# Where in SBUF the halves of the weights lie, modulo 256 bytes, in a hybrid attention and S5 block

## The chip, the cores and the metric

The kernel runs on one core of one Trainium2 chip. The metric is the time of one execution in device microseconds (us), as the median of several runs.

## The reference

One decoder block over 256 tokens of width 1024, all in float32:

```
h = rms_norm(x, norm_mix_g)
q, k, v, u, g = split(h @ w_in)          # 8 heads of 128; u: 512 wide; g: two gates of 1024
o_a = causal softmax attention(rotary(q), rotary(k), v)   # 256 tokens are one MoBA block
o_b = s5_branch(u)                       # complex diagonal scan, gelu, then GLU with w_glu
mixed = sigmoid(g_a) * o_a + sigmoid(g_b) * o_b
x = x + mixed @ w_out
h = rms_norm(x, norm_mlp_g)
x = x + square(relu(h @ w_up)) @ w_down  # 1024 -> 4096 -> 1024
return rms_norm(x, norm_final_g)
```

## The kernel before

Every large product keeps float32 precision by splitting both factors into two halves in the matmul type float32r: hi is a copy in that type, made by ScalarE (line 88), and lo is the rest, made by VectorE (line 89). A product is then three matmuls, hi by hi, hi by lo and lo by hi.

The weights come in units of 128 x 1024 float32 (512 KB). A unit is loaded by the SP queue into one of five `raw` buffers and split into one of four `hi` and one of four `lo` buffers. TensorE uses the units in two ways:

- Stationary weights, 256 columns moving (`mm3`, lines 93 to 95, and line 184 for u): q, k and the gates g of the in-projection and the up stage. The 128x128 pieces of the unit are loaded into the array and x's parts, 256 tokens, move. One unit is 24 matmuls.
- Moving weights, 512 columns (`tok_mm`, lines 270 to 272, and `down`, lines 737 to 739): v, the second gate gb, GLU, merge (w_out, tile names wo) and down. Here the activations' parts are the stationary data. One unit is 12 matmuls. In the second half of down the tokens of the second half (tile names dnq) are done in two pieces of 256 columns, 12 more matmuls for 6 of the 512 wide ones.

The activations' halves are: `xgh`, `xgl` (x times its norm's weights) for the in-projection; the same place under the names `x2h`, `x2l` for up; `yhl` for GLU; `mxh`, `mxl` for merge; `hh`, `hl` for down.

The order of units is V, the S5 preparation, q, k and g of four pairs of heads with attention in between, gb, GLU (four units of columns), merge, up (16 pairs of units), down (two halves of 16 units). TensorE takes its instructions in that order, mixed with the matmuls of attention and S5 as a planner has laid them. In up pairs 0 and 1 are interleaved by the planner, from pair 2 on the units follow one another. In the second half of down the last four units are held back (`LAST = 4`) and their pieces ordered by output.

The addresses. Tiles of a pool lie one behind the other in the order of their first use, each rounded up to 32 bytes a partition. `keep` holds, among others, at these bytes of a partition in the compiled program: half_pi 41920, quarter 41952, xgh and x2h 41984, xgl and x2l 50176, the four hi buffers 58368, 62528, 66688 and 70848, the four lo buffers 75008, 79168, 83328 and 87488, mxh 91648, mxl 99840. The pools ph1 and ph2 follow at 108032: yhl 118272, hh 120320, hl 153088. Modulo 256, x's parts, yhl, mxh, mxl, hh and hl are at 0. A hi or lo buffer has 64 bytes more than the data (`SHIFT = 16` float32), so the four hi buffers are at 0, 64, 128 and 192, and the four lo buffers too. The two halves of a unit always have the same place. Each offset inside a tile that a matmul uses is a multiple of 256 bytes (or of 512), so the place of a tile modulo 256 is that of every piece.

Which buffer a unit gets is fixed by the order in which buffers come free. In up from pair 2 on, and in down, the units have the places 64, 192, 0, 128 in turn. The second unit of the second k pair (tile k, from about 86.9 us) has 64.

Of the kernel before, what the change touches and what calls it, by code (L numbers as in the profile page):

```python
# [8 lines left out]
F32 = mybir.dt.float32  # L9
F32R = mybir.dt.float32r  # L10
# [6 lines left out]
P = 128  # L17
# [16 lines left out]
TURN = 2.0 * math.pi  # L34

RAW, HI, LO = 5, 4, 4
SHIFT = 16
SPLIT_PRIO = 800
HEAT = 7
RSP = 600  # L40
# [9 lines left out]
def build(ctx, tc, dr, out):  # L50
    nc = tc.nc
    V, S, G, PE = nc.vector, nc.scalar, nc.gpsimd, nc.tensor

    keep = ctx.enter_context(tc.tile_pool(name="keep", bufs=1))
# [14 lines left out]
    def w_load(src, name):  # L69
        raw = keep.tile([P, 1024], F32, tag="raw", bufs=RAW, name=f"raw_{name}")  # L70
        nc.sync.dma_start(raw, src)
        return raw

    def parts(name):

        return [keep.tile([P, 1024 + SHIFT], F32R, tag=tag, bufs=bufs, name=f"{tag}_{name}")[:, 0:1024]
                for tag, bufs in (("hi", HI), ("lo", LO))]

    def w_unit(src, name, raw=None):
        if raw is None:  # L80
            raw = w_load(src, name)
        hi, lo = parts(name)
        with tc.high_priority(SPLIT_PRIO):
            split(hi, lo, raw)
        return hi, lo

    def split(hi, lo, x):
        ins = S.copy(hi, x).ins  # L88
        V.tensor_sub(lo, x, hi.bitcast(F32))  # L89
        return ins  # L90
# [56 lines left out]
    ident, tri = cst[:, 640:768], cst[:, 768:896]  # L147
    ones = keep.tile([P, 1], F32, name="ones")
    V.memset(ones, 1.0)
    half_pi = keep.tile([P, 1], F32, name="half_pi")  # L150
    V.memset(half_pi, math.pi / 2)
    quarter = keep.tile([P, 1], F32, name="quarter")
    V.memset(quarter, 0.25)
    heat = p1.tile([P, 512], BF16, tag="sw", name="heat")
    V.memset(heat, 0.0)
    hot = att_bank("hot").rearrange("p a b -> p (a b)")
# [3 lines left out]

    xgh = keep.tile([P, KD, T], F32R, tag="xh", name="xgh")
    xgl = keep.tile([P, KD, T], F32R, tag="xl", name="xgl")
    sq = p1.tile([P, KD, T], F32, tag="yhl", name="sq")
    u_acc = ps.tile([P, 2, 2, T], F32, tag="x", name="u_acc")
    for c in range(4):
        wh, wl = parts(f"u{c}")
        for k2 in range(2):
            k, cols = 2 * c + k2, slice(k2 * 512, (k2 + 1) * 512)
            xk = xT[:, k, :] if k else x0
            S.activation(xgh[:, k, :], xk, AF.Copy, scale=g_mix[:, k : k + 1])  # L170
            V.scalar_tensor_tensor(xgl[:, k, :], xk, g_mix[:, k : k + 1],
                                   xgh[:, k, :].bitcast(F32), op0=ALU.mult, op1=ALU.subtract)
            if k:
                last = split(wh[:, cols], wl[:, cols], u_raw[c][:, cols])
                if k == 1:
                    second = last
            else:
                for i in range(2):
                    part = slice(i * 256, (i + 1) * 256)
                    split(wh[:, part], wl[:, part], u_raw[c][:, part])  # L180
            ws = [slice(k2 * 512 + m * P, k2 * 512 + (m + 1) * P) for m in range(4)]
            for i, (w, x) in enumerate(((wh, xgh), (wh, xgl), (wl, xgh))):
                for m in range(4):
                    PE.matmul(u_acc[:, m // 2, m % 2, :], w[:, ws[m]], x[:, k, :],
                              start=(k == 0 and i == 0 and m % 2 == 0),
                              stop=(k == KD - 1 and i == 2), skip_group_check=True)
# [41 lines left out]
    u = p1.tile([P, 4, 2, P], F32, name="u")  # L228
# [18 lines left out]
    def in_unit(i, name):  # L247
        return w_unit(dr["w_in"][i], f"{name}_{i}", early.get(i))
# [356 lines left out]
    for step in ORDER.split():  # L605
# [28 lines left out]
        elif part == "B":  # L634
            for i in range(2):
                thb[2 * n + i] = p1.tile([P, 2, T], F32, tag=("cs", "sn")[n], bufs=4,
                                         name=f"thb{2 * n + i}")
# [10 lines left out]
    for q in range(4):  # L648
        acc = wide_banks(f"glu{q}") if q % 2 else [flat(mm_bank(f"glu{q}{h}")) for h in range(2)]
        for kk_ in range(2):  # L650
            wh, wl = w_unit(dr["w_glu"][2 * q + kk_], f"glu{q}{kk_}")
            for k2 in range(2):
                k, w = 2 * kk_ + k2, slice(k2 * 512, (k2 + 1) * 512)
                for hf in range(2):
                    tok_mm(acc[hf], wh[:, w], wl[:, w], yhl[0][:, 0:4], yhl[0][:, 4:8], k, hf,
                           k == 0, k == 3)
        tp = att_bank(f"mt{q}")
        for hf in range(2):
            sg = p1.tile([P, T], F32, tag=f"ab{hf}", name="sg")
            act(sg, acc[hf][:, 256:512], AF.Tanh, scale=0.5)  # L660
            V.scalar_tensor_tensor(sg, sg, 1.0, acc[hf][:, 0:256], op0=ALU.add, op1=ALU.mult)
            tb = thb[q][:, hf, :]
            V.scalar_tensor_tensor(tb, tb, 1.0, sg, op0=ALU.add, op1=ALU.mult)
            for i in range(2):
                PE.transpose(tp[:, i, hf * P : (hf + 1) * P], tb[:, i * P : (i + 1) * P], ident)
        two = slice(2 * q, 2 * q + 2)
        V.scalar_tensor_tensor(mixA[:, two, :], tp, 0.5, mixA[:, two, :],
                               op0=ALU.mult, op1=ALU.add)
        split(mxh[:, two, :], mxl[:, two, :], mixA[:, two, :])
# [12 lines left out]
    for c in range(2):  # L682
        acc = wide_banks(f"wo{c}") if c else [flat(mm_bank(f"wo{c}{h}")) for h in range(2)]
        for kk_ in range(4):
            wh, wl = w_unit(dr["w_out"][c, kk_], f"wo{c}{kk_}")
            for k2 in range(2):
                k, w = 2 * kk_ + k2, slice(k2 * 512, (k2 + 1) * 512)
                for hf in range(2):
                    tok_mm(acc[hf], wh[:, w], wl[:, w], mxh, mxl, k, hf, k == 0, k == KD - 1)
        tps = [att_bank(f"xt{c}{i}") for i in range(2)]  # L690
        for hf in range(2):
            xc = x2t[:, hf, c * 512 : (c + 1) * 512]
            V.scalar_tensor_tensor(xc, acc[hf], 0.5, xc, op0=ALU.mult, op1=ALU.add)
            for i in range(4):
                PE.transpose(tps[i // 2][:, i % 2, hf * P : (hf + 1) * P],
                             xc[:, i * P : (i + 1) * P], ident)
        for i in range(4):
            m, tp = 4 * c + i, tps[i // 2][:, i % 2, :]
            S.activation(x2h[:, m, :], tp, AF.Copy, scale=g_mlp[:, m : m + 1])
            V.scalar_tensor_tensor(x2l[:, m, :], tp, g_mlp[:, m : m + 1],  # L700
                                   x2h[:, m, :].bitcast(F32), op0=ALU.mult, op1=ALU.subtract)
# [70 lines left out]
    for c in range(2):  # L772
# [4 lines left out]
        for kk_ in range(16):  # L777
            wh, wl = w_unit(dr["w_down"][c, kk_], f"dn{c}{kk_}")
# [105 lines left out]
```

## Time and profile before

| | |
|---|---|
| median of 3 runs | 403.47 us (402.77 to 404.03) |
| the profiled execution | 403.71 us |
| its span, first to last instruction | 401.9 us |
| mean granted TensorE clock (share of full speed) | 0.999 |
| busy: TensorE matmul / weight loads | 391.6 us / 351.2 us |
| busy: VectorE / ScalarE / GpSimd | 292.6 / 226.0 / 29.2 us |

A profile is of one execution, and its times count from the first instruction. Matmuls are pipelined: a matmul's record lasts two to three times as long as the time until the next one starts, so the busy time of TensorE says little on its pace. The pace is read from the starts.

### The profile page before, as it was taken

How to read it: one execution, taken by the hardware profiler on the slowest of the kernel's cores; microseconds unless marked ns; L12 is line 12 of the kernel's file. 1: busy time of each engine (PE TensorE's matmuls, PEld its weight loads, DVE VectorE, ACT ScalarE, POOL GpSimd, SP SyncE). 2: the span in 40 equal slices, each digit the busy share in tenths (PEclk: the TensorE clock that was granted, in tenths of full speed). 3: DMA queues.
4: the chain of work that ended last, by engine and by line, in shares of the span. 5: the costliest groups of instructions: out<-in, count | busy, mean ns of one | idle time of the engine just before them, and what ended most of it. 6: DMA issues, size and time to landing. Idle time of an engine off the chain costs nothing.

```text
span 401.9 us, 6862 instructions
## 1 busy us (share of the span) xinstructions
PE 391.6 (97%) x2635; PEld 351.2 (87%) x2635; DVE 292.6 (73%) x520; ACT 226.0 (56%) x360; POOL 29.2 (7%) x39
## 2 busy tenths in 40 slices
PE   7999999999999999999999999999999999999993
PEld 4988898989899787888889999999999888899983
DVE  4999999999999994769739675666666444563425
ACT  6867977655276557845647656465555434344323
POOL 4251491000000000000000000000000000000000
PEclk9999999999999999999999999999999999999999
DMA  7994843354616263446486465555655455564202
GB/s 223 402 347 145 247 155 104 106 207 135 208 57 208 78 200 104 161 158 206 157 309 205 129 250 185 181 190 177 204 170 205 166 202 184 181 210 169 94 0 104
DMA packets 23199, 71.57 MB, mean 178 GB/s; under 512 B 2944, under 2 KB 5248, under 8 KB 23168
## 3 DMA queue, kind: packets, MB, share of 16 engines
q1 hardware_dynamic: 20144, 68.92, 50.5%
q10 hardware_dynamic: 3024, 2.23, 1.9%
q8 instruction: 20, 0.33, 0.3%
q14 instruction: 11, 0.09, 0.1%
HBM read 69.18 MB, written 1.05 MB: 175 GB/s over the span
## 4 chain that ended last, share of the span: by engine, by line
PE 74%; DVE 11%; DMA 6%; issue 3%; ACT 2%; POOL 2%; ACTq 1%; SPq 0%; DVEq 0%
PE up L94 8%; PE up L95 8%; PE up L93 7%; PE dn L739 6%; PE dn L737 6%; PE dn L738 6%; DMA x2t<-x 2%; PE gb L272 2%; PE gb L270 2%; PE dnq L737 2%; PE dnq L738 2%; PE dnq L739 2%; PE gb L271 2%; PE glu L270 2%; PE glu L272 2%
## 5 line engine op out<-in xcount | busy, mean ns | idle before, releaser
L94 PE MATMUL up<-x2l,hi_up 128*128 128x256 f32 x256 | 71.8, 281 | 0.1
L95 PE MATMUL up<-x2h,lo_up 128*128 128x256 f32 x256 | 71.7, 281 | 0.0
L93 PE MATMUL up<-x2h,hi_up 128*128 128x256 f32 x256 | 71.3, 281 | 0.0
L89 DVE TENSOR_TENSOR lo_dn<-raw_dn,hi_dn 128x1024 fp32r<-128x1024 f32 x32 | 39.2, 1225 | 43.9 <-ACT hi_dn L88 43.9
L88 ACT CAST hi_dn<-raw_dn 128x1024 fp32r<-128x1024 f32 x32 | 33.6, 1049 | 51.5 <-PE dn L739 25.4
L89 DVE TENSOR_TENSOR lo_up<-raw_up,hi_up 128x1024 fp32r<-128x1024 f32 x32 | 38.8, 1224 | 26.5 <-ACT hi_up L88 26.5
L88 ACT CAST hi_up<-raw_up 128x1024 fp32r<-128x1024 f32 x32 | 33.3, 1048 | 38.1 <-PE up L94 18.1
L94 PEld LDWEIGHTS up<-x2l,hi_up 128*128 128x128 f32 x256 | 48.5, 189 | 0.3 <-DVE x2l L700 0.3
L95 PEld LDWEIGHTS up<-x2h,lo_up 128*128 128x128 f32 x256 | 48.3, 189 | 0.0
L93 PEld LDWEIGHTS up<-x2h,hi_up 128*128 128x128 f32 x256 | 48.1, 189 | 0.1
L739 PE MATMUL dn<-hi_dn,hl 128*128 128x512 f32 x96 | 37.8, 394 | 0.0
L737 PE MATMUL dn<-hi_dn,hh 128*128 128x512 f32 x96 | 37.8, 394 | 0.0
L738 PE MATMUL dn<-lo_dn,hh 128*128 128x512 f32 x96 | 37.7, 393 | 0.0
L739 PEld LDWEIGHTS dn<-hi_dn,hl 128*128 128x128 f32 x96 | 18.0, 188 | 4.1
L738 PEld LDWEIGHTS dn<-lo_dn,hh 128*128 128x128 f32 x96 | 18.1, 188 | 3.6
L737 PEld LDWEIGHTS dn<-hi_dn,hh 128*128 128x128 f32 x96 | 18.0, 188 | 3.6
L94 PE MATMUL g<-xgl,hi_g 128*128 128x256 f32 x64 | 18.7, 292 | 0.0
L93 PE MATMUL k<-xgh,hi_k 128*128 128x256 f32 x64 | 18.2, 285 | 0.0
L95 PE MATMUL g<-xgh,lo_g 128*128 128x256 f32 x64 | 18.2, 284 | 0.0
L95 PE MATMUL q<-xgh,lo_q 128*128 128x256 f32 x64 | 18.2, 284 | 0.0
L95 PE MATMUL k<-xgh,lo_k 128*128 128x256 f32 x64 | 18.1, 283 | 0.0
L93 PE MATMUL g<-xgh,hi_g 128*128 128x256 f32 x64 | 18.1, 283 | 0.0
(267 smaller groups left out, 1040.7 us busy)
## 6 DMA issues: line engine op xcount, KB each, us to landing
raw_up<-w_up SPq DMA_DIRECT2D x32, 512.0 KB, 3.3
raw_dn<-w_down SPq DMA_DIRECT2D x32, 512.0 KB, 3.3
raw_v<-w_in SPq DMA_DIRECT2D x8, 512.0 KB, 6.0
raw_q<-w_in SPq DMA_DIRECT2D x8, 512.0 KB, 3.7
raw_k<-w_in SPq DMA_DIRECT2D x8, 512.0 KB, 3.3
raw_g<-w_in SPq DMA_DIRECT2D x8, 512.0 KB, 4.0
raw_gb<-w_in SPq DMA_DIRECT2D x8, 512.0 KB, 3.8
raw_glu<-w_glu SPq DMA_DIRECT2D x8, 512.0 KB, 3.3
```

The costliest lines, as they stand in the source:

```text
L88: ins = S.copy(hi, x).ins
L89: V.tensor_sub(lo, x, hi.bitcast(F32))
L93: PE.matmul(o, wh, xh, start=first, stop=False, **kw)
L94: PE.matmul(o, wh, xl, start=False, stop=False, **kw)
L95: PE.matmul(o, wl, xh, start=False, stop=last, **kw)
L270: PE.matmul(acc, xh[:, k, rows], wh, start=first, stop=False)
L271: PE.matmul(acc, xh[:, k, rows], wl, start=False, stop=False)
L272: PE.matmul(acc, xl[:, k, rows], wh, start=False, stop=last)
L737: PE.matmul(acc, xh, wh[:, w], start=(k == 0), stop=False, skip_group_check=True)
L738: PE.matmul(acc, xh, wl[:, w], start=False, stop=False, skip_group_check=True)
L739: PE.matmul(acc, xl, wh[:, w], start=False, stop=(k == 31), skip_group_check=True)
```

## The change

The 64 bytes behind each hi and lo buffer go. The tiles of the two constants half_pi and quarter, one column each, get 16 columns of which the first is used, and quarter is allocated, and set, behind xgl in place of ahead of xgh. Nothing else is changed.

```diff
-SHIFT = 16
...
-    def parts(name):
-
-        return [keep.tile([P, 1024 + SHIFT], F32R, tag=tag, bufs=bufs, name=f"{tag}_{name}")[:, 0:1024]
-                for tag, bufs in (("hi", HI), ("lo", LO))]
-
     def w_unit(src, name, raw=None):
         if raw is None:
             raw = w_load(src, name)
-        hi, lo = parts(name)
+        hi = keep.tile([P, 1024], F32R, tag="hi", bufs=HI, name=f"hi_{name}")
+        lo = keep.tile([P, 1024], F32R, tag="lo", bufs=LO, name=f"lo_{name}")
...
-    half_pi = keep.tile([P, 1], F32, name="half_pi")
+    half_pi = keep.tile([P, 16], F32, name="half_pi")[:, 0:1]
     V.memset(half_pi, math.pi / 2)
-    quarter = keep.tile([P, 1], F32, name="quarter")
-    V.memset(quarter, 0.25)
...
     xgh = keep.tile([P, KD, T], F32R, tag="xh", name="xgh")
     xgl = keep.tile([P, KD, T], F32R, tag="xl", name="xgl")
+
+    quarter = keep.tile([P, 16], F32, name="quarter")[:, 0:1]
+    V.memset(quarter, 0.25)
...
     for c in range(4):
-        wh, wl = parts(f"u{c}")
+        wh = keep.tile([P, 1024], F32R, tag="hi", bufs=HI, name=f"hi_u{c}")
+        wl = keep.tile([P, 1024], F32R, tag="lo", bufs=LO, name=f"lo_u{c}")
```

## Rows read from the trace of the kernel before

**Rows 1.** The page: busy time of TensorE, and two costliest groups.

```profile
PE 391.6 (97%) x2635; PEld 351.2 (87%) x2635; DVE 292.6 (73%) x520; ACT 226.0 (56%) x360; POOL 29.2 (7%) x39
...
L94 PE MATMUL up<-x2l,hi_up 128*128 128x256 f32 x256 | 71.8, 281 | 0.1
...
L739 PE MATMUL dn<-hi_dn,hl 128*128 128x512 f32 x96 | 37.8, 394 | 0.0
```

**Rows 2.** The chain of waits: shares; pieces by start us, us, what.

```profile
PE 74%; DVE 11%; DMA 6%; issue 3%; ACT 2%; POOL 2%; ACTq 1%; SPq 0%; DVEq 0%
...
74.60 1.10 DVE lo_q L89
...
200.70 9.02 DMA x2t<-x
...
214.99 0.39 PE up L94
```

**Rows 3.** Waits of TensorE: us in total, times, longest us.

```profile
PE hot L158 <- DVE heat L155: 1.3, 1, 1.3
```

**Rows 4.** Timeline of TensorE, up: first matmuls of seven successive units (start us, us).

```profile
227.08 0.28 PE L93 MATMUL up<-x2h,hi_up 128*128 128x256 f32 x1
...
229.81 0.28 PE L93 MATMUL up<-x2h,hi_up 128*128 128x256 f32 x1
...
232.53 0.28 PE L93 MATMUL up<-x2h,hi_up 128*128 128x256 f32 x1
...
235.41 0.28 PE L93 MATMUL up<-x2h,hi_up 128*128 128x256 f32 x1
...
238.25 0.28 PE L93 MATMUL up<-x2h,hi_up 128*128 128x256 f32 x1
...
241.08 0.28 PE L93 MATMUL up<-x2h,hi_up 128*128 128x256 f32 x1
...
243.90 0.28 PE L93 MATMUL up<-x2h,hi_up 128*128 128x256 f32 x1
```

**Rows 5.** Timeline, down's first half: unit starts, two inside the third, last row second half.

```profile
306.45 0.40 PE L737 MATMUL dn<-hi_dn,hh 128*128 128x512 f32 x1
...
309.25 0.39 PE L737 MATMUL dn<-hi_dn,hh 128*128 128x512 f32 x1
...
312.05 0.40 PE L737 MATMUL dn<-hi_dn,hh 128*128 128x512 f32 x1
...
312.75 0.39 PE L737 MATMUL dn<-hi_dn,hh 128*128 128x512 f32 x1
...
314.79 0.40 PE L737 MATMUL dn<-hi_dn,hh 128*128 128x512 f32 x1
...
317.58 0.40 PE L737 MATMUL dn<-hi_dn,hh 128*128 128x512 f32 x1
...
350.88 0.40 PE L737 MATMUL dn<-hi_dn,hh 128*128 128x512 f32 x1
```

**Rows 6.** Timeline, down's second half: third unit's start, its successor's, and the fifth's.

```profile
356.45 0.39 PE L737 MATMUL dn<-hi_dn,hh 128*128 128x512 f32 x1
...
359.26 0.39 PE L737 MATMUL dn<-hi_dn,hh 128*128 128x512 f32 x1
...
362.08 0.39 PE L737 MATMUL dn<-hi_dn,hh 128*128 128x512 f32 x1
```

**Rows 7.** Timeline, one unit of k at place 64: ends of two runs.

```profile
87.78 0.28 PE L95 MATMUL k<-xgh,lo_k 128*128 128x256 f32 x1
...
89.14 0.28 PE L95 MATMUL k<-xgh,lo_k 128*128 128x256 f32 x1
...
90.16 0.28 PE L94 MATMUL k<-xgl,hi_k 128*128 128x256 f32 x1
...
90.75 0.28 PE L93 MATMUL q<-xgh,hi_q 128*128 128x256 f32 x1
```

**Rows 8.** Windows, line 93 alone: stretch, us, busy us (matmuls), clock, DMA share, GB/s.

```profile
79.00:166.00 87.00, 33.23 (x118) 1.00 0.45 144
```

## The prediction, made before the result was known

> **What bounds the kernel now.** I read the page first: TensorE is busy 97% of the span, and the two groups that cost most are the up matmuls (three lines of 256) and the down matmuls [rows 1]. Then the chain of waits: 74% of it is TensorE. Up to about 79 us the chain runs over VectorE and transfers (the last long VectorE piece stands at 74.60), from there to the end over TensorE, with one hole: at 200.70 it goes over the transfer of x2t, and comes back to TensorE with the up stage at 214.99 [rows 2]. The view of waits has little for TensorE: the longest total is 1.3 us, ahead of the warm-up matmuls [rows 3]. So no wait is there to remove. What sets the time from 79 us on is how far apart TensorE starts its matmuls, and a change of addresses can act on that alone.
>
> So the third view is the timeline of TensorE, read by start times, not by durations, since matmuls overlap. In the up stage a unit of weights is 24 matmuls of 256 columns. From pair 2 on the units lie, in turn, 64, 192, 0 and 128 bytes behind x's parts, modulo 256. The starts of seven successive units [rows 4] give the step, as the difference of two starts over 24:
> pair 2: at 64, 2.73 us, 113.8 ns; at 192, 2.72 us, 113.3 ns. Pair 3: at 0, 2.88 us, 120.0 ns; at 128, 2.84 us, 118.3 ns. Pair 4: at 64, 2.83 us, 117.9 ns; at 192, 2.82 us, 117.5 ns.
> Nothing differs between these units but the place. Two things are to be seen. Distance 0 costs 120 ns and 128 costs 118.3. And distances 64 and 192 have two levels, 113.3 and near 118: within a run each level holds (48 matmuls in pair 2, 48 in pair 4), and which one a run gets is settled at its entry.
>
> The down stage has 512 columns, 12 matmuls a unit, and the weights move. Its first four units, at 64, 192, 0 and 128, take 2.80, 2.80, 2.74 and 2.79 us. Inside the unit at 0 the first three steps take 312.05 to 312.75, 233 ns each, and the last nine 312.75 to 314.79, 226.7 ns each [rows 5]. The whole first half is 350.88 - 306.45 = 44.43 us for 192 matmuls, 231.4 ns a step.
>
> **The change part by part.** No instruction is added or removed: the memsets of the two constants write the same column, quarter's comes a few instructions later on VectorE, and its reader is the first table of angles, far behind; I cost this at nothing (a memset is well under the 1.3 us that the warm-up waits for VectorE, and that hides it). What moves is addresses. From the addresses before (tiles are rounded to 32 bytes) those after follow: half_pi grows from 32 to 64 bytes and quarter leaves, so xgh stays at 41984, place 0. Quarter's 64 bytes stand behind xgl at 58368, so hi begins at 58432, place 64, and with buffers of 4096 bytes all eight stay there. mxh comes to 91200, place 64. Both phase pools begin 448 bytes lower, which takes yhl, hh and hl from place 0 to place 64.
>
> So in-projection, u and up (weights against x's parts) run always at distance 64, and GLU, merge and down always at distance 0. Terms:
>
> Up, pairs 2 to 15: 306.45 - 227.08 = 79.37 us for 672 matmuls, 118.1 ns [rows 4, 5]. At the level of 113.3 with a few steps to enter it: 672 x 113.4 = 76.2, gain 3.2 us. At the slow level of 64: 672 x 117.9 = 79.2, gain 0.15. Pairs 0 and 1 (96 matmuls) stand among waits for x2h; of the 96 x 4.7 = 0.45 I take 0.2.
>
> Which level? The rows show entries at 64 both ways: fast at 227.08, slow at 238.25 [rows 4]; in one unit of k at 64 the run from 87.78 to 89.14 has 12 steps in 1.36 us (113.3) and, after matmuls of another kind came between, that from 90.16 to 90.75 five in 0.59 (118) [rows 7]. Two and two. After the change the up stage has one buffer place, so nothing in the order of units throws a run off its level: one entry, after the last transposes of x2, decides nearly all of 80 us. I take the fast level as the likeliest, because the slow rows of pair 4 come straight out of distance 128, which is gone, and the fast 192 unit of pair 2 shows that a fast run goes on over a unit's border. It is little better than even.
>
> Down, first half: 192 x 226.7 = 43.5 plus some 0.05 us for the steps until it settles: gain 0.85 us. If 226.7 is not held, the whole unit at distance 0, 2.74 us, gives 228.3 ns, a gain of 0.6.
>
> Down, second half: the quarters are 256 wide, at distance 0, and lose. The first four units take 350.88 to 362.08, 2.80 us each; the one at 0 takes 356.45 to 359.26, 2.81 us [rows 5, 6]. 16 x 0.01 = 0.16, and I take 0.2 us lost. By the fully slow 120 ns, 192 x (120 - 117.5) = 0.5 would be lost.
>
> GLU and merge: 96 matmuls each, 512 wide, now at distance 0 and cut up by transposes that start the settling again: from 231.4 to some 229.4, 0.2 us for GLU. Merge's gain partly ends in the wait for x2t's transfer (9.02 us in the chain, [rows 2]), so 0.1. Bounds: nothing, and 192 x 4.7 = 0.9.
>
> In-projection, 256 wide: 118 matmuls of each of the three lines from 79 to 166 us, 354 in all [rows 8]. Attention matmuls break them up, so both levels will occur; the fast one everywhere would give 354 x 4.7 = 1.7, the slow one everywhere nothing. I take 0.3 gained. What lies ahead of 79 us I cost at nothing: VectorE's chain covers it; without that cover it would be up to 222 x 4.7 = 1.0. The 512-wide v and gb units keep the distance that their 64 buffers have now, 2.80 us in the down unit of that distance against a mean of 2.78: nothing. The fp32 transposes against the identity in cst change their distance; cst stays and their data moves; by the code 76 matmuls, at the 7 ns between the extreme steps of [rows 4] 0.5 us either way, taken as nothing.
>
> Sum: 3.2 + 0.2 + 0.85 - 0.2 + 0.2 + 0.1 + 0.3 = 4.65 us. The profiled execution took 403.71 us (span 401.9 and 1.8 around it): 403.71 - 4.65 = 399.06, so 399.1 us. The median before, 403.47, is 0.24 lower; I leave the forecast where it is.
>
> The weight load that runs beside a matmul reads the next weights while the data moves, and the rows give one form of matmul steps from 113.3 to 120.0 ns by place alone [rows 4]. The Trainium skill, on the page "TensorE: Matmul & The Clock Gate" (section "Step-by-step: what each phase is for"), says that TensorE has two independent read ports, so that loading the next weights steals no read bandwidth from the running matmul; by that rule place would be indifferent. The rows don't agree with it. The same page (section "Wait — 56ns, not 53.3ns?") gives a warm step as columns over 2.4 GHz plus 2.5 ns, 109.2 ns at 256; no row here reaches it, and an estimate by it would be 672 x 8.9 = 6.0 us gained in up.
>
> **The rivals.**
> The slow level: the up stage enters at 117.9 and stays there. For it: rows at 238.25 and 90.16. Against: those at 227.08 and 87.78. Up gains 0.15 in place of 3.4, the in-projection nothing, down 0.65 in all, GLU and merge 0.3: 403.71 - 1.1 = 402.6 us. A stage that changes level midway would end near 401.
>
> No effect of place: the differences belong to the order of units, not to their addresses. For it only that two levels exist at one distance. Against: 0 is always slow. 403.7 us.
>
> Slower: the change doesn't do what it says, and weights come to x's own place, distance 0, as they would if a tile's rounding took up the 64 bytes. Then up runs at 120 throughout: 768 x 1.9 = 1.5 us lost, in-projection 354 x 1.9 = 0.7, while down gains 0.65 and GLU and merge 0.3: 403.71 + 2.2 - 0.95 = 404.9 us. Against it: half_pi and quarter lie 32 bytes apart now. The sum turns to a loss once 500 of these 1,122 matmuls run at 120 (0.95 us over 1.9 ns).
>
> **How the numbers follow.** Fast level 0.50; changing midway 0.10; slow level 0.27; no effect 0.04; slower 0.09. About 0.3% (1.2 us, so 402.3 and 404.7) is what a measurement of this kernel can tell from no change. Faster: 0.50 + 0.10 + 0.08 of the slow level = 0.68. Same: 0.19 + 0.04 = 0.23. Slower 0.09. The likeliest case has its own range, 397.6 (1.4 more in the in-projection) to 400.2 (nothing in GLU, merge and in-projection, 0.6 in down's first half, 0.5 lost in its quarters). The range to 403.2 takes in midway and slow and leaves out no effect, slower and a little beside.
>
> **What would show it.** In the timeline after, the up units should all be 2.72 us long, with no 2.88 in every fourth; one length of 2.83 everywhere is the slow level. Mean durations of the up lines fall with the step. In down's first half every unit should be 2.72 from the second on, and the quarters' 12 matmuls 1.43 each. The prediction is wrong if up units differ among themselves, if down stays at 2.78, or if TensorE waits where it now doesn't.

## The result and the profile after

The changed kernel takes 398.2 us (median of its first runs; 397.78 to 399.6) where the kernel before, beside it, takes 403.55 us: ratio 0.9868 [0.9848, 0.9887]. A second measurement gave 398.11 against 403.37, ratio 0.9873 [0.9857, 0.9889]. The forecast was 399.1 us, faster.

The execution of the changed kernel that was profiled first ran at a granted TensorE clock of 0.755 and took 482.88 us; it is left out, and the rows of after come from a second profile of the same kernel, an execution of 398.29 us (span 396.5, clock 0.995).

The page of the profile after, busy time and the costliest group of the same name, to be read against [rows 1]:

```profile
PE 387.9 (98%) x2635; PEld 350.0 (88%) x2635; DVE 292.4 (74%) x520; ACT 225.9 (57%) x360; POOL 31.0 (8%) x39
...
L89 PE MATMUL up<-x2l,hi_up 128*128 128x256 f32 x256 | 70.6, 277 | 0.0
```

The instruction counts of every engine are those of before. The mean record of this up matmul falls from 281 to 277 ns; from pair 2 on its step falls from 118.1 to 113.3. A record does not give the step: it lasts 2.4 times as long in up, and in down, before, 394 ns for a step of 231, which is 1.7 times and not two to three. So the reading has to go by starts.

The chain of waits after (start us, us, what), with its shares by engine, to be read against [rows 2]:

```profile
PE 81%; DVE 8%; ACT 3%; POOL 2%; DMA 2%; issue 2%; ACTq 0%; SPq 0%
...
213.71 0.24 PE up L88 x2
213.95 0.12 PE up L89
```

The transfer of x2t is no longer a piece of it: the chain reaches the third matmul of up (213.95) from the second, without a gap, where before it came to it from VectorE and the transfer. The view of waits (us in total, times, longest us) still begins with the warm-up, as [rows 3] did:

```profile
PE hot L151 <- DVE quarter L158: 1.2, 1, 1.2
```

The view names quarter's memset only because it now ends last on VectorE. The warm-up reads heat alone, and starts 0.06 us behind the end of heat's memset in both kernels (before 0.94 + 0.27, start 1.27; after 0.92 + 0.27, start 1.25), so the change adds no wait there.

The timeline of TensorE after (start us, us, engine, line, operation, tile, shapes, count): the first matmuls of GLU, merge and up; up's third and fifth; the last transposes of x2 and two starts 33 steps apart; the two units' starts of pair 2; down's start, its second unit, its second half; in that half the first of twelve 256-wide matmuls and the 512-wide one behind them.

```profile
165.58 0.47 PE L267 MATMUL glu<-hi_glu,yhl 128*128 128x512 f32 x1
...
190.11 0.39 PE L267 MATMUL wo<-hi_wo,mxh 128*128 128x512 f32 x1
...
213.55 0.40 PE L88 MATMUL up<-x2h,hi_up 128*128 128x256 f32 x2
213.79 0.28 PE L89 MATMUL up<-x2l,hi_up 128*128 128x256 f32 x1
...
214.02 0.28 PE L88 MATMUL up<-x2h,hi_up 128*128 128x256 f32 x1
...
216.97 1.04 PE L692 MATMUL xt<-cst,x2t 128*128 128x128 f32 x8
...
218.08 0.28 PE L88 MATMUL up<-x2h,hi_up 128*128 128x256 f32 x1
...
221.82 0.28 PE L88 MATMUL up<-x2h,hi_up 128*128 128x256 f32 x1
...
225.45 0.28 PE L88 MATMUL up<-x2h,hi_up 128*128 128x256 f32 x1
...
228.17 0.28 PE L88 MATMUL up<-x2h,hi_up 128*128 128x256 f32 x1
...
301.61 0.39 PE L734 MATMUL dn<-hi_dn,hh 128*128 128x512 f32 x1
...
304.35 0.39 PE L734 MATMUL dn<-hi_dn,hh 128*128 128x512 f32 x1
...
345.14 0.39 PE L734 MATMUL dn<-hi_dn,hh 128*128 128x512 f32 x1
...
352.14 0.28 PE L734 MATMUL dnq<-hi_dn,hh 128*128 128x256 f32 x1
...
353.58 0.40 PE L734 MATMUL dn<-hi_dn,hh 128*128 128x512 f32 x1
```

And five rows of the kernel before that [rows 4] and [rows 5] leave out, in the same columns: the first matmuls of GLU, merge and up, up's fifth matmul, and the last transposes of x2.

```profile
166.01 0.47 PE L270 MATMUL glu<-hi_glu,yhl 128*128 128x512 f32 x1
...
190.76 0.40 PE L270 MATMUL wo<-hi_wo,mxh 128*128 128x512 f32 x1
...
214.51 0.39 PE L93 MATMUL up<-x2h,hi_up 128*128 128x256 f32 x2
...
215.32 0.28 PE L93 MATMUL up<-x2h,hi_up 128*128 128x256 f32 x1
...
218.27 1.03 PE L695 MATMUL xt<-cst,x2t 128*128 128x128 f32 x8
```

What is to be seen. The up unit from 225.45 takes 2.72 us, and so do all 28 from pair 2 on: 301.61 - 225.45 = 76.16 us for 672 steps, 113.3 ns. The fast level begins at the last transposes of x2: the 25 steps ahead of them, from 214.02 to 216.97, take 118 ns each, and right behind them the step is 3.74 / 33 = 113.3. In down the unit is 2.74, and the first half 43.53 us, 226.7 a step. The quarters (the 256-wide pieces, dnq) are slow, as expected: 1.44 us for twelve, 120 ns. Stage by stage, from these starts and [rows 4, 5]:

| stretch | before, us | after, us | gain | forecast |
|---|---|---|---|---|
| to GLU's start | 166.01 | 165.58 | 0.43 | 0.3 |
| GLU | 24.75 | 24.53 | 0.22 | 0.2 |
| merge, to up's start | 23.75 | 23.44 | 0.31 | 0.1 |
| up, pairs 0 and 1 | 12.57 | 11.90 | 0.67 | 0.2 |
| up, pairs 2 to 15 | 79.37 | 76.16 | 3.21 | 3.2 |
| down, first half | 44.43 | 43.53 | 0.90 | 0.85 |
| down, second half, to the span's end | 51.02 | 51.36 | -0.34 | -0.2 |
| sum | 401.9 | 396.5 | 5.40 | 4.65 |

### The profile page after: what moved, and what is told of

Same layout as the page of the kernel before. It is cut to its first block, busy times and chain, and to the rows that moved or that the text cites. A ratio compares the mean times of both kernels' runs of the same rounds, so it can differ in the third digit from the quotient of the medians.

```text
span 481.1 us, 6862 instructions
## 1 busy us (share of the span) xinstructions
PE 473.2 (98%) x2635; PEld 404.8 (84%) x2635; DVE 294.9 (61%) x520; ACT 227.6 (47%) x360; POOL 29.5 (6%) x39
## 4 chain that ended last, share of the span: by engine, by line
PE 98%; ACT 1%; DMA 1%; DVE 0%; issue 0%
PE up L89 8%; PE up L90 8%; PE up L88 7%; PE dn L735 6%; PE dn L734 6%; PE dn L736 6%; PE u_acc L181 3%; PE k L88 2%; PE v L269 2%; PE q L88 2%; PE q L90 2%; PE g L90 2%; PE wo L267 2%; PE g L88 2%; PE gb L267 2%; PE gb L268 2%
## 5 line engine op out<-in xcount | busy, mean ns | idle before, releaser
L89 PE MATMUL up<-x2l,hi_up 128*128 128x256 f32 x256 | 80.5, 315 | 0.0
L90 PE MATMUL up<-x2h,lo_up 128*128 128x256 f32 x256 | 79.9, 313 | 0.0
L88 PE MATMUL up<-x2h,hi_up 128*128 128x256 f32 x256 | 79.6, 314 | 0.0
L90 PEld LDWEIGHTS up<-x2h,lo_up 128*128 128x128 f32 x256 | 56.9, 222 | 0.0
L88 PEld LDWEIGHTS up<-x2h,hi_up 128*128 128x128 f32 x256 | 56.5, 221 | 0.2
L89 PEld LDWEIGHTS up<-x2l,hi_up 128*128 128x128 f32 x256 | 56.6, 221 | 0.0
L735 PE MATMUL dn<-lo_dn,hh 128*128 128x512 f32 x96 | 44.0, 458 | 0.0
L736 PE MATMUL dn<-hi_dn,hl 128*128 128x512 f32 x96 | 43.9, 457 | 0.0
L89 PE MATMUL q<-xgl,hi_q 128*128 128x256 f32 x64 | 20.4, 319 | 0.0
L88 PE MATMUL q<-xgh,hi_q 128*128 128x256 f32 x64 | 20.2, 316 | 0.0
```

Source lines behind the costliest of these rows:

```text
L88: PE.matmul(o, wh, xh, start=first, stop=False, **kw)
L89: PE.matmul(o, wh, xl, start=False, stop=False, **kw)
L90: PE.matmul(o, wl, xh, start=False, stop=last, **kw)
L735: PE.matmul(acc, xh, wl[:, w], start=False, stop=False, skip_group_check=True)
L736: PE.matmul(acc, xl, wh[:, w], start=False, stop=(k == 31), skip_group_check=True)
```

## The experiments

The theory: what counts is the distance modulo 256 between the weights' parts and the activations' parts, and at 64 and 192 the matmuls that lead into up choose one of two levels, which then holds. The rivals: the absolute place counts, or the order of units, or one distance has one price. Each kernel is the changed one with the edit shown, but for the two by stage: they are the kernel before, its two constants where they were, with the function shown in place of its own. None leaves out any of the computation; where matmuls are added, what they write is overwritten by the stage that follows. Medians and ratios are against the kernel before on the same chip. Rows are of TensorE's timeline, columns as above: the first matmul of pair 2 of up and the first of down, and what else the text speaks of.

**The changed kernel again.** No edit.

> The changed kernel once more, for a profile at the full clock. Theory (distance modulo 256 sets the step, and up holds one of two levels): 398.2 us; every up unit of 24 matmuls takes 2.72 us (113.3 ns a step) from the first to the last; units of down's first half take 2.72 us (226.7 ns) from the second on, the quarters' 12 matmuls 1.43 us. Rival (up holds the slow level, 2.83 us a unit, and the gain is elsewhere, in the in-projection, merge or waits): up stage no shorter than before (79.4 us for pairs 2 to 15), some 5 us found elsewhere.

398.11 us (397.67 to 398.88, four executions), ratio 0.9873 [0.9857, 0.9889]. Its rows are those above.

**The 64 bytes away.** Both constants as in the kernel before, ahead of x's parts, but buffers without their extra 64 bytes: all eight at distance 0 in every stage. It is also the "slower" rival of the prediction made into a kernel.

```diff
-    half_pi = keep.tile([P, 16], F32, name="half_pi")[:, 0:1]
+    half_pi = keep.tile([P, 1], F32, name="half_pi")
     V.memset(half_pi, math.pi / 2)
+    quarter = keep.tile([P, 1], F32, name="quarter")
+    V.memset(quarter, 0.25)
...
-    quarter = keep.tile([P, 16], F32, name="quarter")[:, 0:1]
-    V.memset(quarter, 0.25)
```

> All weight buffers at one place, but x's own (distance 0 everywhere, no 64 bytes between them). Theory (distance counts): 256-wide steps 120 ns in up and in-projection, 672 up matmuls 80.6 us, down's 512-wide steps 226.7: up to 4.5 us more than the changed kernel in up, 2 in the in-projection, 404.5 us. Rival (what counts is that all buffers lie at one place, so that no change of place throws a run off its level): within 1 us of the changed kernel, 398 to 399 us.

404.31 us, ratio 1.0024 [1.0011, 1.0037].

```profile
226.94 0.28 PE L88 MATMUL up<-x2h,hi_up 128*128 128x256 f32 x1
...
307.58 0.40 PE L734 MATMUL dn<-hi_dn,hh 128*128 128x512 f32 x1
```

80.64 us for the same 672 matmuls, 120.0 ns. So one place for all buffers is not the gain; which place it is decides, on either side of the kernel before.

**The weights at 192, and at 128.** One number each.

```diff
-    quarter = keep.tile([P, 16], F32, name="quarter")[:, 0:1]
+    quarter = keep.tile([P, 48], F32, name="quarter")[:, 0:1]    # 192
+    quarter = keep.tile([P, 32], F32, name="quarter")[:, 0:1]    # 128, the other kernel
```

> All weight buffers 192 bytes behind x's parts, the other stationary data at the weights' place as in the change. Theory (64 and 192 alike have the two levels 113.3 and 117.9, the entry decides): either 398 us with up units of 2.72 us, or 402 with 2.83. Rival (64 alone is good): 402 us or more, with steps that no unit at 192 had before.

> All weight buffers 128 bytes behind x's parts, the other stationary data at the weights' place. Theory: up at 118.3 (or at 120, which one disturbed k unit at 128 held), in-projection near 118.3, the rest as in the changed kernel: 402.5 to 404 us, and one level only. Rival (64 is one of several places that are all good, only 0 is bad): 398 us.

At 192: 402.58 us (ten executions, 401.69 to 403.19), ratio 0.9981 [0.9972, 0.9991].

```profile
227.37 0.28 PE L88 MATMUL up<-x2h,hi_up 128*128 128x256 f32 x1
...
306.51 0.40 PE L734 MATMUL dn<-hi_dn,hh 128*128 128x512 f32 x1
```

At 128: 403.93 us, ratio 1.0014 [1.0, 1.0029].

```profile
227.53 0.29 PE L88 MATMUL up<-x2h,hi_up 128*128 128x256 f32 x1
...
308.17 0.40 PE L734 MATMUL dn<-hi_dn,hh 128*128 128x512 f32 x1
```

79.14 us (117.8 ns) at 192, from the same instructions that reach 113.3 at 64; and 80.64 at 128, the 120.0 ns of distance 0. The 118.3 of the unit at 128 in [rows 4] was not what 128 costs once it is undisturbed; it stood between units at other places.

**The activations at 0, the weights at 64 all through.** The constants are laid so that yhl, mxh, mxl, hh and hl are at place 0 again: down's distance becomes 64, up's stays.

```diff
-    ones = keep.tile([P, 1], F32, name="ones")
-    V.memset(ones, 1.0)
-    half_pi = keep.tile([P, 16], F32, name="half_pi")[:, 0:1]
+    half_pi = keep.tile([P, 24], F32, name="half_pi")[:, 0:1]
...
+    ones = keep.tile([P, 48], F32, name="ones")[:, 0:1]
+    V.memset(ones, 1.0)
```

> The weights stay 64 behind x's parts, but GLU's, merge's and the MLP's stationary data go back to place 0, so that moving weights stand 64 behind the stationary data. Theory: up and in-projection as in the changed kernel; down's first half at 229 (or 233) ns a step, 0.4 to 1.3 us more, GLU and merge 0.2 to 0.5 more, quarters at 113 or 118 instead of 119.5, 0.2 to 1.2 us less: 397.7 to 399.7 us. Rival (a good part of the gain is in GLU, merge and down): 400 us or more.

Ten executions fall in two groups: 397.05, 397.11, 397.23 and 397.44, and six from 401.06 to 402.23, all at a granted clock of 0.993 to 0.999. The median is 401.34, ratio 0.9919 [0.9882, 0.9955]. The execution of 397.44 is the profiled one.

```profile
225.47 0.28 PE L88 MATMUL up<-x2h,hi_up 128*128 128x256 f32 x1
...
301.63 0.39 PE L734 MATMUL dn<-hi_dn,hh 128*128 128x512 f32 x1
...
345.58 0.39 PE L734 MATMUL dn<-hi_dn,hh 128*128 128x512 f32 x1
```

Up has the fast length, 76.16. Down's first half takes 43.95 us, 228.9 ns a step, so distance 0 is worth 0.42 us there against 64. Down's second half, to the end of the span of 395.7, takes 50.1 us, 1.2 less than in the changed kernel, so for down as a whole distance 64 was the better one here. The two groups lie some 4 us apart, the price of up's two levels (2.98) and something more. That one program has both levels in up is the nearest reading, but it is not shown: no execution of the other group was profiled.

**Everything moved by 64.** x's parts at 64, all the rest at 128, the distances as in the changed kernel.

```diff
-    half_pi = keep.tile([P, 16], F32, name="half_pi")[:, 0:1]
+    half_pi = keep.tile([P, 32], F32, name="half_pi")[:, 0:1]
```

> The changed kernel with x's parts 64 bytes further as well: x's parts at place 64, weights and the other stationary data at 128. All distances are those of the change, all places others. Theory (the distance alone counts): the same steps, 113.3 in up (or, if the entry falls so, 117.8), 226.7 in down's first half; 398 us. Rival (the place itself counts): up at 118.3 as the weights' place 128 had before, 402 us or more.

Executions of 398.44 (the profiled one), 400.41, 401.14, 401.31 and 403.18 us; ratio 0.9944 [0.9909, 0.9979].

```profile
225.60 0.28 PE L88 MATMUL up<-x2h,hi_up 128*128 128x256 f32 x1
...
301.76 0.39 PE L734 MATMUL dn<-hi_dn,hh 128*128 128x512 f32 x1
```

Again 76.16 us in the profiled execution. Weights at place 128, which took 120.0 ns at distance 128, take 113.3 here at distance 64, so the step goes with the distance and not with the weights' place. But the median is 3 us above that of the changed kernel and above the 398 expected, so at the same distances the level is not sure; whether the place has a part in which level comes is not shown.

**The distance by stage.** Buffers 64 columns longer, at place 0; a unit starts in column 16 (64 bytes) where x or the quarters move over it, in column 0 for the stages that gain at distance 0. It should also take back the loss in the quarters.

```diff
+    def parts(name):
+        far = name[0] in "uqk" or name[0:2] in ("g_", "dn") and name[0:3] != "dn0"
+        c0 = 16 if far else 0
+        return [keep.tile([P, 1024 + 64], F32R, tag=tag, bufs=4, name=f"{tag}_{name}")[:, c0 : c0 + 1024]
+                for tag in ("hi", "lo")]
```

> Buffers of 4352 bytes at place 0; each stage picks its distance by starting 0 or 64 bytes into them: 64 for u, q, k, g, up and down's second half, 0 for v, gb, GLU, merge and down's first half. Theory: up at 113.3 if the entry falls so, down's first half at 226.7, second half at 229 and 113.3 (1.2 us less than the changed kernel), gb at 226.7 (0.2 less): 396.7 us, or 401 with the slow level in up. Rival (the distance of the second half makes no difference there): 398 us, second half as long as in the changed kernel.

400.96 us: 398.56, 398.85 and four from 400.66 to 401.49 (the profiled one); ratio 0.9928 [0.9902, 0.9954].

```profile
226.14 0.28 PE L93 MATMUL up<-x2h,hi_up 128*128 128x256 f32 x1
...
305.29 0.40 PE L738 MATMUL dn<-hi_dn,hh 128*128 128x512 f32 x1
```

Here up at 64 had the slow length, 79.15: the two lengths seen at 192 and at 64 are the same two. Down's second half, from 348.83 to the end of the span of 399.7, takes 50.9 us, 0.5 less than in the changed kernel where 1.2 was expected. What it wins is lost many times over where up falls on the wrong level.

**Six matmuls ahead of pair 2.** If the entry chooses the level, a few matmuls at distance 0 should change it. Six matmuls of x's parts with themselves were added at the code's place for pair 2, in the kernel with 192, and in the one with the activations at 0.

```diff
+        if i == 2:
+            for _ in range(6):
+                PE.matmul(acc[:, 0, :], x2h[:, 0, 0:P], x2h[:, 0, :], start=True, stop=True)
```

> The kernel with the weights 192 behind x's parts, which held 117.8 ns through up, plus six matmuls of x2h by x2h (256 columns, distance 0, results overwritten) in the second pair of up. Before, each undisturbed passage from distance 0 to 192 fell to 113.3. Theory (two levels at 192, the entry decides): the six cost 0.7 us, after them up holds 113.3 ns to its end: some 3 us saved, net 2.3 us less than without them, near 400.3 us. Rival (192 gives 117.8 in a program of this kind, whatever the entry): 0.7 us more, near 403.3 us.

> The same six matmuls in the kernel with the stationary data back at 0, whose executions came out at 397.1 to 397.4 or at 401.1 to 402.2 us. Theory (two levels in up, the entry decides): with one and the same entry all executions fall together, at 398 (six matmuls cost 0.7, 113.3 held) or at 402.5. Rival (the two groups come from something else, a wait or a transfer): both groups stay, 0.7 us later each.

At 192: 403.1 us, ratio 0.9996 [0.9983, 1.0008], not the 400.3 that the theory gave.

```profile
214.71 0.88 PE L711 MATMUL up<-x2h 128*128 128x256 f32 x6
215.43 0.28 PE L89 MATMUL up<-x2l,hi_up 128*128 128x256 f32 x1
...
217.70 0.28 PE L88 MATMUL up<-x2h,hi_up 128*128 128x256 f32 x1
217.82 0.38 PE L692 MATMUL xt<-cst,x2t 128*128 128x128 f32 x2
...
227.30 0.28 PE L88 MATMUL up<-x2h,hi_up 128*128 128x256 f32 x1
...
306.44 0.39 PE L737 MATMUL dn<-hi_dn,hh 128*128 128x512 f32 x1
```

The planner set the six at 214.71, ahead of the last transposes of x2. Behind them are twenty steps in 2.27 us, 113.5 ns, at a distance that had shown 117.8; then come the transposes, and from 227.30 the 79.14 us of the slow level. The lead-in did work, and the transposes undid it. The other kernel gave 398.22 us (397.58 to 398.68, four executions), ratio 0.9876 [0.9861, 0.9891]:

```profile
214.64 0.28 PE L89 MATMUL up<-x2l,hi_up 128*128 128x256 f32 x1
...
217.00 0.28 PE L88 MATMUL up<-x2h,hi_up 128*128 128x256 f32 x1
...
226.32 0.28 PE L88 MATMUL up<-x2h,hi_up 128*128 128x256 f32 x1
...
302.48 0.39 PE L737 MATMUL dn<-hi_dn,hh 128*128 128x512 f32 x1
```

Fast, 76.16, and the executions fall together, though four are few. It is not the six that made it fast: the twenty steps behind them, from 214.64 to 217.00, take 118.0 ns, and the 113.3 begins only behind the last transposes of x2. So at distance 64 the six brought the slow level and the transposes the fast one, the reverse of what they did at 192.

**The six behind the transposes.** The same, reading other pieces of x's parts (the last to be ready), so that they stand exactly between pairs 1 and 2; in the kernel with 192, which should become fast, and in the changed kernel, which should become slow.

```diff
+        if i == 2:
+            for _ in range(6):
+                PE.matmul(acc[:, 0, :], x2h[:, KD - 1, 0:P], x2l[:, KD - 1, :], start=True, stop=True)
```

> The kernel with the weights 192 behind x's parts, with six matmuls at distance 0 (256 columns, results overwritten) between up's pairs 1 and 2, so behind the last transposes of x2. Theory (the level is set at the entry and kept): pairs 0 and 1 at 117.8, the six at 120, then 672 matmuls at 113.3 ns; 0.7 us spent, 3.0 saved against 402.6: 400.3 us, in all executions. Rival (something in the stage itself, transfers or the other engines, holds 117.8): 403.3 us.

> The changed kernel with the same six matmuls at the same spot; a passage from distance 0 to 64 fell to 118 in the one run that had it. Theory (the changed kernel's 113.3 hangs on the entry alone): after the six, up holds 117.9 to its end, 0.7 + 3.1 us more than the changed kernel, 401.9 us. Rival (distance 64 in the changed kernel returns to 113.3 by itself): 398.8 us.

At 192: 400.19 us (399.63 to 400.74), ratio 0.9919 [0.9895, 0.9943].

```profile
224.36 0.28 PE L88 MATMUL up<-x2h,hi_up 128*128 128x256 f32 x1
...
226.12 0.88 PE L711 MATMUL up<-x2l,x2h 128*128 128x256 f32 x6
226.84 0.28 PE L88 MATMUL up<-x2h,hi_up 128*128 128x256 f32 x1
...
303.00 0.39 PE L737 MATMUL dn<-hi_dn,hh 128*128 128x512 f32 x1
```

The changed kernel with the six: 402.63 us, ratio 0.9977 [0.9963, 0.9991].

```profile
224.32 0.28 PE L88 MATMUL up<-x2h,hi_up 128*128 128x256 f32 x1
...
225.68 0.88 PE L711 MATMUL up<-x2l,x2h 128*128 128x256 f32 x6
226.40 0.28 PE L88 MATMUL up<-x2h,hi_up 128*128 128x256 f32 x1
...
305.54 0.39 PE L737 MATMUL dn<-hi_dn,hh 128*128 128x512 f32 x1
```

This pair decides. At 192 the last fifteen steps ahead of the six take 1.76 us, 117.3 ns, and the 672 behind them 76.16, 113.3 ns. At 64 it is twelve steps in 1.36 us, 113.3, and then 79.14 us, 117.8. The same six matmuls, 0.72 us of work, turn the level both ways, and it stays turned for nearly 80 us. So neither level belongs to a distance, and the order of units has no part in it. That the six do this by their distance 0, and not as any six matmuls put there would, was not tried. The changed kernel with this entry has the up stage of the "slow level" rival; that its 402.63 meets the rival's 402.6 is chance, for 0.72 us of it is the six.

**The distance by stage, with three late matmuls.** The kernel of the distance by stage again, with up and the second half of down at 192 and three late matmuls in place of six.

```diff
+        c0 = 48 if name[0:2] == "up" or name[0:3] == "dn1" else 16 if name[0] in "uqk" or name[0:2] == "g_" else 0
...
+        if i == 2:
+            for _ in range(3):
+                PE.matmul(acc[:, 0, :], x2h[:, KD - 1, 0:P], x2l[:, KD - 1, :], start=True, stop=True)
```

> Distance by stage: 64 for u, q, k and g, 0 for v, gb, GLU, merge and down's first half, 192 for up and down's second half, and three matmuls at distance 0 between up's pairs 1 and 2. Theory: up 113.3 from pair 2 on in all executions, down's first half 226.7, second half as the 192 units before (232.5 and 114.3 ns, 0.8 us less than the changed kernel), gb 0.1 less, lead-in 0.4 more, pairs 0 and 1 0.4 more: 398 us, and no execution beyond 399. Rival (the levels still vary by execution): a spread of 3 us or more.

401.43 us, ratio 0.9948 [0.9932, 0.9964].

```profile
225.91 0.52 PE L714 MATMUL up<-x2l,x2h 128*128 128x256 f32 x3
226.27 0.28 PE L92 MATMUL up<-x2h,hi_up 128*128 128x256 f32 x1
...
305.41 0.40 PE L740 MATMUL dn<-hi_dn,hh 128*128 128x512 f32 x1
```

The quarters gained what was expected, 1.36 us for twelve (355.87 to 357.23, 113.3 ns) in place of 1.44. Up did not: 79.14, and no execution came below 400.79, where none beyond 399 was expected. That three are too few where six were enough is the nearest reading; the in-projection's distance differs too between the two kernels, so it isn't shown. Six in this kernel were not tried, and no version tried here is reliably faster than the changed kernel.

## Why the prediction was right

**That the distance sets the pace** was right, with one limit: at 64 and 192 it sets which two levels there are, and not which of them comes. With everything moved by 64 the profiled length of up stays 76.16, while moving the weights alone gives 76.16, 79.14 or 80.64. The rival "no effect of place" falls by the kernel at distance 0: the order of units is that of the changed kernel, the median 6.2 us higher. That kernel, 404.31, also bears out the price of the "slower" rival (the sum written there, 403.71 + 2.2 - 0.95, gives 404.96 and not 404.9). The 118.3 ns that the prediction read for distance 128 was too low: 120.0 where nothing else mixes in.

**Up, pairs 2 to 15**, 3.2 forecast, 3.21 measured. The two levels were read rightly from [rows 4] and [rows 7], and that a level holds over 672 steps was right. That one entry, after the last transposes of x2, decides was right too. The reason given for the fast level (that the slow rows of pair 4 come out of distance 128) does not hold: in the changed kernel, with no unit at 128, the steps ahead of those transposes are slow as well (118 ns), and six matmuls put behind pair 1 turn the level. So that the fast level came was in part luck, and near even odds were fair to what the rows showed. Afterwards all nine executions of the changed kernel at full clock lie between 397.67 and 399.6, while the kernels with the same distance in up, with the activations at 0, with everything moved by 64 and with the distance by stage, had executions 3 to 5 us apart. What the traces add is where the entry is made: in the changed kernel the step is 118 ahead of the transposes and 113.3 behind them; in the profile of the same code with six late matmuls it is 113.3 ahead of them (nine steps from 216.06 to 217.08) and 113.3 behind; in the kernel by stage it is 118 on both sides. Why they leave the changed kernel at the fast level each time is open.

**Pairs 0 and 1** were mis-sized: 0.2 of the possible 0.45 was taken, and 0.67 came. The first two matmuls take two steps; before, the third starts 214.99 - 214.51 = 0.48 us after the first, and after the change 213.79 - 213.55 = 0.24. So 0.24 was a wait: the chain before comes to that third matmul from VectorE's x2l, and to that from the transfer of x2t [rows 2]. The step behind it is late too, and by the fifth matmul the wait cost 0.34 (215.32 - 214.51 against 214.02 - 213.55). It is gone, as the chain after shows, and in the view of transfers x2t's takes 8.1 us in place of 9.02. That goes with the execution and not with the change, and was luck for the sum: in the profile of the same code with six late matmuls the transfer took 9.13 us and the third matmul came 0.94 us behind the first (213.05, 213.99). The 25 steps from the fifth matmul to the last transposes gained nothing, 2.95 us before and after (118 ns). From the transposes to pair 2 it is 8.81 us before and 8.48 after: 0.33 gained by the step, between the 0.2 taken and the possible 0.45.

**GLU** 0.22 for 0.2. That distance 0 gave it is not shown: in the kernel with the activations at 0, at distance 64, GLU took 24.52 us (165.60 to 190.12), no more than here. **Merge** 0.31 for 0.1: the step that failed is "partly ends in the wait for x2t's transfer". In the profiled execution there was no such wait, and the gain stayed whole; that the wait can be there is said above.

**In-projection and what is ahead** 0.43 for 0.3, on the way between its two bounds. The size is no firmer than one execution: the same code with six late matmuls starts GLU at 165.13, 0.45 us ahead of 165.58.

**Down, first half** 0.90 for 0.85: 226.7 ns from the second unit on, as the last nine steps of one unit in [rows 5] had shown. That this is the distance and not something else of the first half follows from the kernel with down at 64, 228.9. **Second half** -0.34 for -0.2: in the quarters the fully slow 120 ns of the bound came true, and the 512-wide matmuls between them gained too little to pay for it (the six ahead of 352.14 take 1.38 us, 230 ns a step).

**The two-port rule.** The Trainium skill ("TensorE: Matmul & The Clock Gate", section "Step-by-step: what each phase is for") has two independent read ports, and a weight load that steals no bandwidth from the matmul. The same 672 matmuls, each with its load, at a granted clock of 0.99 or more, took 76.16, 79.14 or 80.64 us by the place of their data and by what ran just ahead; the measurements decide against indifference to place, without showing what causes it. The estimate of 109.2 ns at 256 columns by the formula of the same page of the Trainium skill (section "Wait — 56ns, not 53.3ns?") was reached by no run: the best level is 113.3.

## What to carry to other kernels

Where TensorE's matmuls run back to back and nothing waits, read the pace from the starts and group them by the address of their two operands modulo 256: here that was worth 1.3% without an instruction changed, with distance 64 for 256-wide and 0 for 512-wide matmuls. In up the runs do not tell 256 from 128: distances 0 and 128 gave the same length, 64 and 192 the same two, and none that is not a multiple of 64 was tried. Do not take a pace that a run of matmuls happens to have for the price of its distance: repeat the execution, and look at what ran just ahead. A few matmuls at the entry of a long stage can be worth more than they cost (0.72 us for 2.98 here, and the other way round), so what runs between stages, transposes too, belongs in the comparison.

## What was not expected of the hardware

The 672 up matmuls came out at three lengths and no other in the twelve kernels with one place for up's units, one profiled execution of each: 76.16, 79.14 (once 79.15) and 80.64 us, 113.3, 117.8 and 120.0 ns a step. Distances 0 and 128 gave only the last in these kernels, 64 and 192 only the first two.

Such a level is kept: behind six matmuls it held for 672 steps, through 28 units with nothing to bring it back. At the last eight fp32 transposes of x2 it turned either way: at distance 192 from 113.5 to 117.8 ns, at 64 from 118 to 113.3, in the changed kernel and in the one with the activations at 0 and six matmuls ahead.

One program, at a granted clock of 0.993 or more, had executions in two groups some 4 us apart (397.05 to 397.44, and 401.06 to 402.23), which in any one run would have passed for an effect of the edit.
